# Moving a per-head multiplication from GpSimd to DVE, inverting in place, and normalizing a chunk earlier, in the projection of a gated DeltaNet layer

## The chip, the cores and the metric

One Trainium2 chip; the program runs on one core. The metric is device time in microseconds (us), the median of the runs shown. Layer 0, both expert layers and the final norm are in the same program as the part that is changed.

## The reference, cut to what matters

The model has two layers and a sequence of 2048 tokens with 1024 features. Layer 1 is a chunked gated DeltaNet with 8 heads of dimension 128. What the change touches is its first stage, up to the chunkwise scan:

```python
def gated_deltanet_mixer(h, w_in, conv_w, a_log, dt_bias, onorm_g, w_out):
    u = h @ w_in                                   # h = rmsnorm(x) * (1 + scale) + shift
    qkv = silu(causal_depthwise_conv(u[..., :3 * DN_WIDTH], conv_w))
    ...
    o = chunk_gated_delta_rule(l2norm(q), l2norm(k), v, beta, g)
    ...
def chunk_gated_delta_rule(q, k, v, beta, g):      # chunks of 64 tokens
    ...
    g = cumsum(g)                                  # within a chunk
    decay = where(causal, exp(g[:, None] - g[None, :]), 0)
    lower = where(strict, (k * beta) @ k.T * decay, 0)
    t_mat = triangular_solve(lower + eye, eye)     # the inversion
    u = t_mat @ (v * beta)
    w = t_mat @ (k * beta * exp(g))
    a_intra = where(causal, q @ k.T * decay, 0)
    qg = q * exp(g)
    kd = k * exp(g_last - g)
    ...                                            # scan over the chunks
```

## The kernel before, in words

`mixer1` runs `dn_project` and then `dn_chain`. `dn_project` makes, for all heads, what the scan needs, and stores it in HBM (the buffer `stg`); `dn_chain` loads it and scans. The sequence is worked off in two halves of 1024 tokens, and a half in two chunks of 512. For each chunk `norm_T` (L202 to L229) loads four tiles of x (128 tokens each, L1141), squares them on ScalarE (L212), makes the reciprocal root on DVE and GpSimd (`rstd`), scales the tiles on DVE (L219), transposes them on the tensor engine (L225), and splits the result into a high and a low part (nf L227, hh L228 on ScalarE, hl L229 on DVE), since every large product is done in three passes (high·high, high·low, low·high). Then `gates` makes beta and the decays of the half, ending in gh and gl (L1086) and in egd, an HBM copy of the cumulated exponentials.

After that `dn_head` (L1178 to L1297) runs for the 8 heads of the half:

- **Decays:** four products of the triangle `upper` with the head's column of g on GpSimd (gm, L1236, four buffers), each taken by the tensor engine (L1238) into a PSUM tile tk, ScalarE's exponential into dt (L1241) and a triangular mask on GpSimd (L1242).
- **Strips:** `strip(1)`, `strip(0)`, `strip(2)` project k, q and v: 48 matrix products of 128x512 each (L256 to L258), an eviction on ScalarE into ub (L1203), a causal filter of four taps on DVE (L1209, L1211, into dacc), and SiLU on ScalarE into kq (L1216; k and q side by side) or vT (L1214). The weights are split by ScalarE (wh) and DVE (wl, L234). After each strip `pump` emits two steps of an inversion, if one is under way, and a piece of the modulation of later layers (modw, mod; L168 and L169 on DVE).
- **Norms:** k and q are transposed by blocks (L1221), squared and summed; kd is made on DVE (L1261).
- **kg:** egb, the head's row of egd spread over all partitions, is loaded into the buffer that ub has used (L1267). kg = kq · egb is one GpSimd multiplication of 128x2048 (L1269), and is stored.
- **strip(3)** projects the output gate (zs, L1201).
- **The block of products:** for each of four pairs of 128-token blocks, kq is split (kqh on ScalarE, kql on DVE, L234), six products of 128x256 (L1281) fill a PSUM tile tp (two buffers), and DVE multiplies the tile by dt into na (L1282). na holds `lower` and `a_intra`. Its diagonal 32x32 pieces go to HBM (`ndia`), and the transposed v is evicted as vp (L1295).

After each four heads `dn_invert` (L1299 to L1318) inverts their diagonal pieces, 31 steps of a multiplication (L1312) and a sum (L1313) on DVE, which grow from 1 to 31 columns. Its generator is advanced by `pump`, two steps per strip, during the next four heads; the last one runs in `dn_chain`. The pieces are loaded into nblk, and the inverse grows in xblk; both come from the four buffers of the x tiles (tag "xin").

The order on each engine is not written out: a scheduler of the tile framework sets it from the program's order, the dependences and the buffers. The engines are in order, and so is SyncE (SP), which issues nearly all DMAs.

Of the kernel before, what the change touches and what calls it, by code (L numbers as in the profile page):

```python
# [6 lines left out]
F32 = mybir.dt.float32  # L7
F32R = mybir.dt.float32r
# [8 lines left out]
P = 128  # L17
# [53 lines left out]
class Trunk:  # L71
# [127 lines left out]
                nc.tensor.transpose(p[:, j * P:(j + 1) * P], src[:, k:k + 1].to_broadcast([P, P]), self.ident)  # L199
            nc.scalar.activation(out[:, h * 512:(h + 1) * 512], p, AF.Copy)  # L200

    def norm_T(self, l, which, xload, psum, wk, outs):  # L202


        nc = self.nc
        hh, hl = outs
        ss = self.small.tile([P, 4], F32, name="ss")
        xs = []
        for i in range(4):
            x = xload(i)  # L210
            sq = wk.tile([P, D], BF16, name="sq", tag="nf", bufs=2)
            nc.scalar.activation(sq, x, AF.Square, accum_out=ss[:, i:i + 1])  # L212
            xs.append(x)
        r = self.rstd(ss, 1.0 / D, 4, "rs")
        for i in range(4):
            if l == 0:
                nc.scalar.activation(xs[i], xs[i], AF.Copy, scale=r[:, i:i + 1])
            else:
                nc.vector.tensor_scalar(xs[i], xs[i], r[:, i:i + 1], None, op0=ALU.mult)  # L219
        g = self.gain[l, which]  # L220
        so = l * 48 + (0 if which == 0 else 3) * 8
        for k in range(KD):
            p = psum.tile([P, 512], F32, name="tp")
            for i in range(4):
                nc.tensor.transpose(p[:, i * P:(i + 1) * P], xs[i][:, k * P:(k + 1) * P], self.ident)  # L225
            f = wk.tile([P, 512], F32, name="nf", bufs=2)
            nc.scalar.activation(f, p, AF.Identity, scale=g[:, k:k + 1], bias=self.mod[:, so + k:so + k + 1])  # L227
            nc.scalar.activation(hh[:, k], f, AF.Copy)  # L228
            nc.vector.tensor_sub(hl[:, k], f, hh[:, k].bitcast(F32))  # L229
# [124 lines left out]
    def mixer0(self, yT, cv, gm):  # L354
        tc, nc, ins = self.tc, self.nc, self.ins
        cin = {}
        with ExitStack() as ctx:
# [4 lines left out]
            wk = ep("wk0", 2)  # L362
# [12 lines left out]
            def xload(c):  # L375
                return lambda i: x0[i] if c == 0 else self.xload0(wk, c * 4 + i)
# [10 lines left out]
            for half in range(2):  # L387
                hT = []
                for c2 in range(2):
                    hh = hp[c2].tile([P, KD, 512], F32R, name="hh")  # L390
                    hl = hp[c2].tile([P, KD, 512], F32R, name="hl")
                    self.norm_T(0, 0, xload(half * 2 + c2), pst, wk, (hh, hl))
                    hT.append((hh, hl))
                if half:
                    self.route_setup(wk)
# [718 lines left out]
    def dn_project(self):  # L1114
# [3 lines left out]
        with ExitStack() as ctx:  # L1118
# [24 lines left out]
                return f  # L1143

            self.rest = self.mod_rest(cv, [(1, i) for i in range(16, 48)], tag="modw", bufs=3)
            for half in range(2):
                hT = []
                ba = cv.tile([P, 8, 16], F32, name="ba", bufs=2)
                for c2 in range(2):
                    hh = hp.tile([P, KD, 512], F32R, name="hh")  # L1150
                    hl = hp.tile([P, KD, 512], F32R, name="hl")
                    self.norm_T(1, 0, xload(half * 2 + c2), pst, wk, (hh, hl))
                    hT.append((hh, hl))
                    p = psm.tile([P, 512], F32, name="pm")
                    self.proj(p[:16], (wbh, wbl), (hh, hl))
                    bs = wk.tile([16, 512], F32, name="bs", bufs=1)
                    nc.scalar.activation(bs, p[:16], AF.Copy)
                    p = pst.tile([P, 512], F32, name="tp")
                    for i in range(4):
                        nc.tensor.transpose(p[:, i * 16:(i + 1) * 16], bs[:, i * P:(i + 1) * P], self.ident[:16, :16])  # L1160
                    nc.vector.tensor_copy(ba[:, c2 * 4:c2 * 4 + 4], p[:, :64].rearrange("p (b c) -> p b c", b=4))
                beta, g, ex = self.gates(half, ba, cv, pst)
                for hd in range(8):
                    self.dn_head(half, hd, hT, beta, g, ex, halo, wp, wk, psm, pst, psk)
                    if hd % 4 == 3:
                        assert next(self.inv, None) is None
                        self.inv = self.dn_invert(half, hd // 4, wk) if (half, hd) != (1, 7) else iter(())
# [8 lines left out]
    def dn_head(self, half, hd, hT, beta, g, ex, halo, wp, wk, psm, pst, psk):  # L1176
# [55 lines left out]
        pe = psk.tile([P, 1024], F32, name="tk")  # L1232
        for c in range(2):
            for i in range(2):
                t = wk.tile([P, 4, P], F32R, name="gm", bufs=4)
                nc.gpsimd.tensor_mul(t, self.upper[:, None, :].to_broadcast([P, 4, P]),  # L1236
                                     g[i][:, hd, c * 4:c * 4 + 4, None].to_broadcast([P, 4, P]))
                nc.tensor.matmul(pe[:, c * 512:(c + 1) * 512], self.slower_r, t.rearrange("p b c -> p (b c)"),  # L1238
                                 start=i == 0, stop=i == 1)
# [25 lines left out]
        nc.gpsimd.tensor_tensor(self.fo[:, hd, half * 8:half * 8 + 8], ssq, self.expo[:, 0:1].to_broadcast([P, 8]), op=ALU.pow)  # L1265
        egb = wk.tile([P, 1024], F32, name="egb", tag="ub", bufs=1)
        nc.sync.dma_start(egb, self.egd[half][hd:hd + 1].to_broadcast([P, 1024]))  # L1267
        kg = self.last.tile([P, 8, 2, P], F32, name="kg", bufs=1)
        nc.gpsimd.tensor_mul(kg, kq, blk(egb)[:, :, None, :].to_broadcast([P, 8, 2, P]))  # L1269
        store(2, 2, kg)  # L1270
        strip(3)
        self.pump(2)
        na = self.last.tile([P, 8, 2, P], F32, name="na", bufs=1)
        for b in range(0, 8, 2):
# [4 lines left out]
            for i in range(2):  # L1279
                for n, (x, y) in enumerate(((kqh, kqh), (kqh, kql), (kql, kqh))):  # L1280
                    nc.tensor.matmul(p[:, i * 256:(i + 1) * 256], x[:, i, 0], y[:, i], start=n == 0, stop=n == 2)  # L1281
            nc.vector.tensor_mul(na[:, b:b + 2], p.rearrange("p (b i c) -> p b i c", b=2, i=2),  # L1282
                                 dt[:, b:b + 2, None, :].to_broadcast([P, 2, 2, P]))
        store(0, 2, na)
        nd, no = self.ndia[half][hd // 4], self.noff[half]
        for sub in range(4):
            dst = bass.AP(tensor=nd.tensor, offset=nd.offset + sub * 32768 + hd % 4 * 1024, ap=[[32, 32], [4096, 8], [1, 32]])
# [7 lines left out]
        nc.vector.tensor_mul(vp, pv, b8(nk))  # L1295
        store(5, 1, vp[:, :, None, :])

    def dn_invert(self, half, hg, wk, bufs=4):


        nc = self.nc
        n = wk.tile([P, 32, 32], F32, name="nblk", tag="xin", bufs=bufs)
        nc.sync.dma_start(n, self.ndia[half][hg])
        x = wk.tile([P, 32, 32], F32, name="xblk", tag="xin", bufs=bufs)
        nc.gpsimd.memset(x, 0.0)
        nc.gpsimd.memset(x.rearrange("p i j -> p (i j)")[:, 0:1024:33], 1.0)
        for j in range(1, 32):
            if j > 1:
                yield
            tmp = wk.tile([P, 32, 32], F32, name="xtmp", tag="sqk", bufs=1)  # L1310
            col = n[:, 0:j, j:j + 1].rearrange("p m o -> p o m").to_broadcast([P, j, j])
            nc.vector.tensor_mul(tmp[:, :j, :j], x[:, :j, :j], col)  # L1312
            nc.vector.tensor_reduce(x[:, 0:j, j:j + 1], tmp[:, :j, :j], axis=AX.X, op=ALU.add, negate=True)  # L1313
        nc.sync.dma_start(self.xinv[half][hg], x)
        xs = self.xsub[half]
        for sub in range(4):
            dst = bass.AP(tensor=xs.tensor, offset=xs.offset + hg * 4096 + sub * 1024, ap=[[8192, 32], [1, 1024]])
            nc.sync.dma_start(dst, x[sub * 32:(sub + 1) * 32].rearrange("p i j -> p (i j)"))  # L1318

    def dn_chain(self, yT):  # L1320
# [3 lines left out]
        with ExitStack() as ctx:  # L1324
# [196 lines left out]
            if True:  # L1521
                both = lambda bl: [load(bl, hg) for hg in range(2)]
                with tc.high_priority(offset=400):
# [2 lines left out]
                    load_n(1)  # L1526
                    both(1)
                    last = load_n(2)
                kg, zs, na, vp = self.stores[-4:]

                def behind(st, ld):
                    tc.add_manual_dep(st.ins, ld.ins.name,
# [10 lines left out]
                        run(*nxt)  # L1543
                for bl in range(16):
                    if bl == 0:
                        self.inv = self.dn_invert(1, 1, iv, 2)
                    if bl + 2 < 16:
                        last = both(bl + 2)[-1]
                    if bl == 0:
# [138 lines left out]
```

## Time and profile before

| | |
|---|---|
| median of 3 runs | 3399.24 us (3396.93 to 3402.08) |
| profiled execution: its time | 3396.98 us |
| profiled execution: span | 3395.2 us |
| mean granted TensorE clock | 0.929 of full speed |
| projection of layer 1 | about 1253 to 2280 us of the span |
| one head (k, q, v, gate strips and the block) | 52.0 to 58.3 us in the stretches read |

How the views are read: a timeline row has start and duration in us, engine, line of the kernel, operation, output<-input, shape, count, and in brackets the idle time of the engine before it with what ended it. PE is the tensor engine, PEld its weight loads, ACT is ScalarE, POOL GpSimd, SP SyncE. A row of waits has the waiting engine and instruction, the instruction waited for, and total us, number and longest. A row of groups has count, busy us and mean ns of one. A row by stretch has the busy time of each engine within it and the TensorE clock that was granted. Durations of matrix products overlap, so the distance from start to start tells their pace.

### The profile page before, as it was taken

Reading aid. Unit: us, or ns where it says so; the run is one execution under the profiler, and the core shown is the slowest. Engines: PE = TensorE matmul, PEld = TensorE weight load, DVE = VectorE, ACT = ScalarE, POOL = GpSimd, SP = SyncE. Lnnn points to the kernel's source line nnn. Section 1 sums busy time; section 2 is a strip of 40 time slices with the busy share of each in tenths; the row PEclk is TensorE's granted clock in tenths of the full one; section 3 lists DMA queues with packets and bytes.
Section 4 is the critical chain, followed back from the end, with each engine's and each line's share of the span. In section 5 each row is a group of like instructions: output and inputs, shape, how many; then the busy total and the mean of one; then the engine's idle time right before and its main releaser. Section 6 shows DMA issues by size and latency. Waiting matters only on the chain. (4 is left out here: it accounts for less than half of the span.)

```text
span 3395.2 us, 41934 instructions
## 1 busy us (share of the span) xinstructions
PE 2939.8 (87%) x14192; PEld 2344.0 (69%) x14192; DVE 2472.0 (73%) x3773; ACT 1492.9 (44%) x2558; POOL 1112.1 (33%) x897
## 2 busy tenths in 40 slices
PE   4979888869999978999878989988998996999991
PEld 3756666547777756877756777767896665777771
DVE  4998998758888856667867685777545656888883
ACT  6134223226565654334334333435663224656552
POOL 1143323333444413242313232244540122344331
PEclk9989989889999989999978999988998997999996
DMA  5216243729999852454432334348757535999875
GB/s 216 92 62 223 77 140 124 248 99 329 302 291 293 272 166 89 139 173 159 164 127 80 98 116 127 100 128 264 230 182 241 174 125 206 308 280 301 268 236 212
DMA packets 384987, 633.40 MB, mean 187 GB/s; under 512 B 111232, under 2 KB 245504, under 8 KB 384768
## 3 DMA queue, kind: packets, MB, share of 16 engines
q1 hardware_dynamic: 355904, 563.38, 48.8%
q0 software_dynamic: 28864, 67.30, 8.4%
q8 instruction: 114, 1.87, 0.2%
q14 instruction: 105, 0.86, 0.1%
HBM read 484.46 MB, written 175.44 MB: 194 GB/s over the span
## 5 line engine op out<-in xcount | busy, mean ns | idle before, releaser
L256 PE MATMUL pm<-hh,wh 128*128 128x512 f32 x1408 | 566.6, 403 | 4.5 <-ACT ub L1203 3.8
L257 PE MATMUL pm<-hl,wh 128*128 128x512 f32 x1408 | 555.6, 395 | 4.2 <-DVE hl L229 4.2
L258 PE MATMUL pm<-hh,wl 128*128 128x512 f32 x1408 | 555.9, 395 | 2.6 <-DVE wl L234 2.6
L234 DVE TENSOR_TENSOR wl<-wr,wh 128x1024 fp32r<-128x1024 f32 x384 | 452.1, 1218 | 41.5 <-ACT wh L233 37.3
L233 ACT ACTIVATE wh<-wr 128x1024 fp32r<-128x1024 f32 x384 | 399.4, 1057 | 126.2 <-PE pu L815 56.5
L834 POOL DMA_INDIRECT acc<-ys,ixs x102 | 264.0, 2588 | 436.4 <-DVE wl L234 132.6
L256 PEld LDWEIGHTS pm<-hh,wh 128*128 128x128 f32 x1408 | 270.3, 192 | 67.4 <-ACT ub L1203 6.3
L257 PEld LDWEIGHTS pm<-hl,wh 128*128 128x128 f32 x1408 | 269.6, 191 | 63.8 <-DVE hl L229 4.6
L258 PEld LDWEIGHTS pm<-hh,wl 128*128 128x128 f32 x1408 | 268.6, 191 | 61.9 <-DVE wl L234 4.7
L234 DVE TENSOR_TENSOR wl<-wraw,wh 128x1024 fp32r<-128x1024 f32 x88 | 133.8, 1520 | 186.6 <-ACT wh L233 186.6
L813 PE MATMUL pu<-wh,xt 128*128 128x512 f32 x656 | 268.6, 409 | 0.5 <-ACT xt L233 0.5
L814 PE MATMUL pu<-wl,xt 128*128 128x512 f32 x656 | 261.0, 398 | 0.0
L815 PE MATMUL pu<-wh,xt 128*128 128x512 f32 x656 | 260.0, 396 | 0.0
L282 DVE SCALAR_TENSOR_TENSOR acc<-cin,wfir,acc 128x512 f32<-128x512 f32 (+1 forms) x320 | 214.8, 727 | 0.1
L532 PE MATMUL po<-woh,yh 128*128 128x512 f32 x512 | 172.4, 413 | 31.5 <-issue 11.3
L1211 DVE SCALAR_TENSOR_TENSOR dacc<-ub,cols,dacc 128x1024 f32<-128x1024 f32 x144 | 188.9, 1312 | 3.0
L233 ACT ACTIVATE wh<-wraw 128x1024 fp32r<-128x1024 f32 x88 | 93.2, 1059 | 219.9 <-PE pm L257 219.8
L532 PE MATMUL po<-wol,yh 128*128 128x512 f32 x512 | 167.0, 406 | 0.0
L532 PE MATMUL po<-woh,yl 128*128 128x512 f32 x512 | 165.7, 403 | 0.2 <-DVE yl L234 0.2
L791 POOL DMA_INDIRECT xg<-hn,ixs x102 | 111.9, 1097 | 162.6 <-PE tp L801 76.5
L189 POOL TENSOR_TENSOR rs<-rs1t,expo 128x1 f32<-128x1 f32 x48 | 28.3, 589 | 383.7 <-DVE rs1t L187 354.6
L815 PEld LDWEIGHTS pu<-wh,xt 128*128 128x128 f32 x656 | 124.0, 189 | 30.8 <-issue 0.3
(377 smaller groups left out, 6520.1 us busy)
## 6 DMA issues: line engine op xcount, KB each, us to landing
wr<-in_w_up_dram SPq DMA_DIRECT2D x256, 512.0 KB
wr<-in_w_down_dram SPq DMA_DIRECT2D x128, 512.0 KB
modw<-in_modwT_dram SPq DMA_DIRECT2D x96, 512.0 KB
wraw<-in_w_in_dram SPq DMA_DIRECT2D x88, 512.0 KB
stin<-stg SPq DMA_DIRECT2D x32, 1280.0 KB
yr<-yT SPq DMA_DIRECT2D x32, 512.0 KB
acc<-xo SPq DMA_DIRECT2D x32, 512.0 KB
hn<-ho SPq DMA_DIRECT2D x32, 512.0 KB
```

The source lines that it names most:

```text
L233: a = nc.scalar.activation(h, x, AF.Copy) if eng == "act" else nc.vector.tensor_copy(h, x)
L234: return a, nc.vector.tensor_sub(l, x, h.bitcast(F32))
L256: nc.tensor.matmul(ps, wh[:, k], hh[:, k], start=k == 0, stop=False)
L257: nc.tensor.matmul(ps, wh[:, k], hl[:, k], start=False, stop=False)
L258: nc.tensor.matmul(ps, wl[:, k], hh[:, k], start=False, stop=k == KD - 1)
L282: self.tap = nc.vector.scalar_tensor_tensor(o, x, w, i, op0=ALU.mult, op1=ALU.add)
L532: nc.tensor.matmul(ps[:, ns], a[:, k], b[:, ns], start=k == 0 and i == 0, stop=k == KD - 1 and i == 2)
L813: nc.tensor.matmul(ps, xh[:, k], uh, start=k == 0, stop=False)
L814: nc.tensor.matmul(ps, xh[:, k], ul, start=False, stop=False)
L815: nc.tensor.matmul(ps, xl[:, k], uh, start=False, stop=k == KD - 1)
L834: st = nc.gpsimd.indirect_dma_start(out=self.acc, out_offset=bass.IndirectOffsetOnAxis(ap=ix[:, 0:1], axis=0), in_=ys, in_offset=None, bou ...
L1211: nc.vector.scalar_tensor_tensor(acc, ub[:, i:i + 1024], self.col("dn_conv", si * 4 + i), acc, op0=ALU.mult, op1=ALU.add)
```

## The change

It has five parts, all in or around `dn_project`.

1. `norm_T` is cut in two: `norm_x` (load, squares, root, scaling) and `norm_T` (transposes and split). For the first chunk of the second half `norm_x` is called before head 7 of the first half.
2. kg is made on DVE, in two multiplications of 128x1024, written behind the loop that makes na, and stored after na.
3. `dn_invert` works in place: the pieces are loaded straight into xblk, which gets a buffer of its own (one) instead of two of the four x tiles. The memset of the whole tile goes; the memset of the diagonal stays and now follows the load.
4. gm has two buffers instead of four.
5. `dn_chain` unpacks the last four stores in their new order (zs, na, kg, vp).

```diff
-    def norm_T(self, l, which, xload, psum, wk, outs):
+    def norm_x(self, l, xload, wk):
         nc = self.nc
-        hh, hl = outs
         ss = self.small.tile([P, 4], F32, name="ss")
...
                 nc.vector.tensor_scalar(xs[i], xs[i], r[:, i:i + 1], None, op0=ALU.mult)
+        return xs
+
+    def norm_T(self, l, which, xs, psum, wk, outs):
+        nc = self.nc
+        hh, hl = outs
...
+            first = None
             for half in range(2):
...
-                    self.norm_T(1, 0, xload(half * 2 + c2), pst, wk, (hh, hl))
+                    xs = first or self.norm_x(1, xload(half * 2 + c2), wk)
+                    first = None
+                    self.norm_T(1, 0, xs, pst, wk, (hh, hl))
...
                 for hd in range(8):
+                    if (half, hd) == (0, 7):
+                        first = self.norm_x(1, xload(2), wk)
                     self.dn_head(half, hd, hT, beta, g, ex, halo, wp, wk, psm, pst, psk)
...
-                t = wk.tile([P, 4, P], F32R, name="gm", bufs=4)
+                t = wk.tile([P, 4, P], F32R, name="gm", bufs=2)
...
-        kg = self.last.tile([P, 8, 2, P], F32, name="kg", bufs=1)
-        nc.gpsimd.tensor_mul(kg, kq, blk(egb)[:, :, None, :].to_broadcast([P, 8, 2, P]))
-        store(2, 2, kg)
         strip(3)
...
         store(0, 2, na)
+        kg = self.last.tile([P, 8, 2, P], F32, name="kg", bufs=1)
+        for b in range(0, 8, 4):
+            nc.vector.tensor_mul(kg[:, b:b + 4], kq[:, b:b + 4], blk(egb)[:, b:b + 4, None, :].to_broadcast([P, 4, 2, P]))
+        store(2, 2, kg)
...
-    def dn_invert(self, half, hg, wk, bufs=4):
+    def dn_invert(self, half, hg, wk):
         nc = self.nc
-        n = wk.tile([P, 32, 32], F32, name="nblk", tag="xin", bufs=bufs)
-        nc.sync.dma_start(n, self.ndia[half][hg])
-        x = wk.tile([P, 32, 32], F32, name="xblk", tag="xin", bufs=bufs)
-        nc.gpsimd.memset(x, 0.0)
+        x = wk.tile([P, 32, 32], F32, name="xblk", bufs=1)
+        nc.sync.dma_start(x, self.ndia[half][hg])
         nc.gpsimd.memset(x.rearrange("p i j -> p (i j)")[:, 0:1024:33], 1.0)
...
-            col = n[:, 0:j, j:j + 1].rearrange("p m o -> p o m").to_broadcast([P, j, j])
+            col = x[:, 0:j, j:j + 1].rearrange("p m o -> p o m").to_broadcast([P, j, j])
```

The scheduler turns this into other orders. The first place is DVE in the block of products of head 1 of the first half. Before (kd, na, wl the low weights of the next strip, kql the low part of k and q, vp):

```order
L1261 TENSOR_TENSOR kd<-tk,kdf 128x1024
L1282 TENSOR_TENSOR na<-tp,dt 128x512
L234 TENSOR_TENSOR wl<-wraw,wh 128x1024
L1282 TENSOR_TENSOR na<-tp,dt 128x512
L234 TENSOR_TENSOR kql<-kq,kqh 128x512 x2
L1295 TENSOR_TENSOR vp<-tk,nk 128x1024
L1282 TENSOR_TENSOR na<-tp,dt 128x512 x2
L234 TENSOR_TENSOR wl<-wraw,wh 128x1024
```

and now (lines from L203 on have moved: L1261 is L1270, L1282 is L1288, L234 is L238, L1295 is L1305, and L1293 is the new kg):

```order
L1270 TENSOR_TENSOR kd<-tk,kdf 128x1024
L1293 TENSOR_TENSOR kg<-kq,egb 128x1024 x2
L1288 TENSOR_TENSOR na<-tp,dt 128x512 x2
L238 TENSOR_TENSOR kql<-kq,kqh 128x512 x2
L1305 TENSOR_TENSOR vp<-tk,nk 128x1024
L1288 TENSOR_TENSOR na<-tp,dt 128x512 x2
L238 TENSOR_TENSOR wl<-wraw,wh 128x1024 x2
```

Both halves of kg stand ahead of the first na, although the program writes them behind the last, and wl stands behind the block.

The second place is the same engine in head 6, with the largest steps of the inversion (xtmp the multiplications, xblk the sums). Before:

```order
L1261 TENSOR_TENSOR kd<-tk,kdf 128x1024
L1313 TENSOR_REDUCE xblk<-xtmp 128x23
L169 TENSOR_TENSOR mod<-mod,cols 128x1
L1312 TENSOR_TENSOR xtmp<-xblk,nblk 128x24x24
L1313 TENSOR_REDUCE xblk<-xtmp 128x24
L1282 TENSOR_TENSOR na<-tp,dt 128x512 x2
L234 TENSOR_TENSOR kql<-kq,kqh 128x512 x2
L1295 TENSOR_TENSOR vp<-tk,nk 128x1024
L1282 TENSOR_TENSOR na<-tp,dt 128x512 x2
```

and now:

```order
L1270 TENSOR_TENSOR kd<-tk,kdf 128x1024
L1322 TENSOR_REDUCE xblk<-xtmp 128x23
L1293 TENSOR_TENSOR kg<-kq,egb 128x1024
L1321 TENSOR_TENSOR xtmp<-xblk 128x24x24
L1288 TENSOR_TENSOR na<-tp,dt 128x512
L1322 TENSOR_REDUCE xblk<-xtmp 128x24
L1288 TENSOR_TENSOR na<-tp,dt 128x512
L238 TENSOR_TENSOR kql<-kq,kqh 128x512 x2
L1293 TENSOR_TENSOR kg<-kq,egb 128x1024
L1288 TENSOR_TENSOR na<-tp,dt 128x512 x2
L1305 TENSOR_TENSOR vp<-tk,nk 128x1024
```

One half of kg and one multiplication of the inversion stand ahead of the first na there, the other half of kg ahead of the last two.

The third place is ScalarE at the start of the first half, where the decays of the half are made (gex and egT are the exponentials in `gates`, dt that of head 0, sq the squares of x tiles, ub the evictions of strips, ACT_TABLE_LOAD a change of function table). Before:

```order
L1203 ACTIVATE ub<-pm 128x512
L233 ACTIVATE wh<-wraw 128x1024
L1079 ACTIVATE gex<-tp 128x192
L1081 ACTIVATE egT<-tp 64x128
L1203 ACTIVATE ub<-pm 128x512
L1241 ACTIVATE dt<-tk 128x1024
L1216 ACT_TABLE_LOAD
L1216 ACTIVATE kq<-dacc 128x8x128
```

and now (L212 is L210, L233 is L237, L1079 is L1083, L1203 is L1212, L1216 is L1225, L1241 is L1250):

```order
L210 ACTIVATE sq,ss<-xin 128x1024 x2
L237 ACTIVATE wh<-wraw 128x1024
L1212 ACTIVATE ub<-pm 128x512
L1225 ACT_TABLE_LOAD
L1225 ACTIVATE kq<-dacc 128x8x128
L1212 ACTIVATE ub<-pm 128x512
L1083 ACT_TABLE_LOAD
L1083 ACTIVATE gex<-tp 128x192
L1085 ACTIVATE egT<-tp 64x128
L1250 ACTIVATE dt<-tk 128x1024
```

The squares of the second half's first chunk, written before head 7, stand here, and so do its four loads and four scalings on SyncE and DVE; the exponentials of the decays now come behind the first strip's SiLU and a further change of table.

More of the change, by code (lines that the diff above doesn't have):

```diff
@@ L391, in mixer0 @@
                     hl = hp[c2].tile([P, KD, 512], F32R, name="hl")
-                    self.norm_T(0, 0, xload(half * 2 + c2), pst, wk, (hh, hl))
+                    self.norm_T(0, 0, self.norm_x(0, xload(half * 2 + c2), wk), pst, wk, (hh, hl))
                     hT.append((hh, hl))
@@ L1528, in dn_chain @@
                     last = load_n(2)
-                kg, zs, na, vp = self.stores[-4:]
+                zs, na, kg, vp = self.stores[-4:]
                 def behind(st, ld):
@@ L1545, in dn_chain @@
                     if bl == 0:
-                        self.inv = self.dn_invert(1, 1, iv, 2)
+                        self.inv = self.dn_invert(1, 1, iv)
                     if bl + 2 < 16:
```

## The prediction, on record before the changed kernel was timed

> **What bounds the kernel now.** I read the page first, then the chain of waits over the projection of layer 1 (1280 to 2300 us), then a timeline of one head, then tables by stretch.
>
> ```profile
> span 3395.2 us, 41934 instructions
> PE 2939.8 (87%) x14192; PEld 2344.0 (69%) x14192; DVE 2472.0 (73%) x3773; ACT 1492.9 (44%) x2558; POOL 1112.1 (33%) x897
> ```
>
> TensorE is busy for 87% of the span, so a gain has to come out of its idle time or its clock. In the waits of the projection these rows touch what the change edits (columns: total us, times, longest us):
>
> ```profile
> PE tp L1281 <- DVE na L1282: 61.4, 15, 5.3
> PE tp L225 <- DVE xin L219: 20.0, 2, 14.2
> POOL kg L1269 <- DMA egb<-egd: 14.6, 14, 2.0
> ```
>
> TensorE waits 61.4 us in 15 waits for na, the eviction of the k·kᵀ and k·qᵀ products, and 14.2 us once for normalized x. Why na is late shows in the timelines of head 6 of the first half, TensorE first, then DVE, then GpSimd:
>
> ```profile
> 1676.50 0.39 PE L258 MATMUL pm<-hh,wl 128*128 128x512 f32 x1
> 1676.73 0.28 PE L1281 MATMUL tp<-kqh 128*128 128x256 f32 x1
> 1676.85 0.28 PE L1281 MATMUL tp<-kql,kqh 128*128 128x256 f32 x1
> ...
> 1678.16 0.71 PE L1221 MATMUL tk<-ident,vT 128*128 128x128 f32 x5
> 1684.08 0.55 PE L1281 MATMUL tp<-kqh 128*128 128x256 f32 x1 [5.22 <-DVE na L1282]
> ...
> 1686.57 0.41 PE L1281 MATMUL tp<-kql,kqh 128*128 128x256 f32 x1
> 1686.78 0.41 PE L1281 MATMUL tp<-kqh,kql 128*128 128x256 f32 x1
> ```
> ```profile
> 1677.13 4.37 DVE L169 TENSOR_TENSOR mod<-mod,cols 128x1 f32<-128x1 f32 x1
> ...
> 1683.26 1.28 DVE L1282 TENSOR_TENSOR na<-tp,dt 128x512 f32<-128x512 f32 x2
> ```
> ```profile
> 1676.95 4.54 POOL L1269 TENSOR_TENSOR kg<-kq,egb 128x2048 f32<-128x2048 f32 x1
> ```
>
> While GpSimd multiplies kg for 4.54 us, a DVE multiplication of one column (L169) takes 4.37 us and ends when kg ends. The group of that line, stretched ones included, has a mean of 335 ns:
>
> ```profile
> L169 DVE TENSOR_TENSOR mod<-mod,cols 128x1 f32<-128x1 f32 x28 | 9.4, 335 | 0.5
> ```
>
> Head 0 shows who is held (GpSimd, then DVE, then TensorE):
>
> ```profile
> 1341.67 4.58 POOL L1269 TENSOR_TENSOR kg<-kq,egb 128x2048 f32<-128x2048 f32 x1 [0.83 <-DMA egb<-egd]
> ```
> ```profile
> 1342.71 0.69 DVE L1282 TENSOR_TENSOR na<-tp,dt 128x512 f32<-128x512 f32 x1 [1.95 <-PE tp L1281]
> 1343.32 4.02 DVE L234 TENSOR_TENSOR wl<-wraw,wh 128x1024 fp32r<-128x1024 f32 x1
> 1347.26 0.68 DVE L1282 TENSOR_TENSOR na<-tp,dt 128x512 f32<-128x512 f32 x1
> 1347.86 1.07 DVE L234 TENSOR_TENSOR kql<-kq,kqh 128x512 fp32r<-128x512 f32 x1
> ```
> ```profile
> 1348.08 0.55 PE L1281 MATMUL tp<-kqh 128*128 128x256 f32 x1 [2.62 <-DVE na L1282]
> ```
>
> na reads PSUM and runs during kg at 0.69; wl has two SBUF inputs and is held until kg ends. DVE works in order, so the second na stands behind the held wl. With two PSUM buffers TensorE then stops for 2.62 us. It pays again afterwards: in head 6 the products stood 0.12 us apart before the gap and 0.21 behind it. The tables by stretch show the clock (a row has the stretch and its length, the busy time and count of PE, PEld, DVE, ACT and POOL, the granted clock, the DMA share and GB/s):
>
> ```profile
> 1347.90:1351.20 3.30, 3.12 (x11) 2.75 (x12) 3.30 (x4) 0.00 (x0) 3.30 (x3) 0.50 1.06 397
> 2241.10:2244.40 3.30, 3.30 (x15) 2.71 (x16) 2.45 (x3) 1.27 (x2) 0.69 (x1) 1.00 0.00 0
> ```
> ```profile
> 2240.99 0.50 PE L256 MATMUL pm<-hh,wh 128*128 128x512 f32 x1 [1.39 <-ACT ub L1203]
> ```
>
> Behind the gap of 2.62 us the granted clock is 0.50 for 3.3 us, which loses 1.65 us of work; behind one of 1.39 us it stays 1.00. So the cost of a block of products is its whole stretch, from the first product to the next strip. For the first 15 heads in one table:
>
> ```profile
> sum 168.20, PE 105.62 PEld 93.52 DVE 154.11 ACT 40.14 POOL 123.57; mean PE 7.04 PEld 6.23 DVE 10.27 ACT 2.68 POOL 8.24
> ```
>
> 168.2 / 15 = 11.2 us each. At full clock TensorE needs about 4.7 (my estimate): 24 products by 0.12, eight transposes by about 0.11 (five took 0.71 with the tail of the last), and four decay products (L1238) as wide as a strip's product, which is 0.23 from start to start (1676.50 to 1676.73).
>
> **The change part by part.** Prices first, from the groups of the projection, and for a DVE product of 1024 elements with two SBUF inputs from the page:
>
> ```profile
> L1269 POOL TENSOR_TENSOR kg<-kq,egb 128x2048 f32<-128x2048 f32 x16 | 73.9, 4617 | 14.8 <-DMA egb<-egd 14.6
> L234 DVE TENSOR_TENSOR kql<-kq,kqh 128x512 fp32r<-128x512 f32 x62 | 47.8, 811 | 23.2 <-ACT kqh L233 23.2
> L1312 DVE TENSOR_TENSOR xtmp<-xblk,nblk 128x961 f32<-128x961 f32 x3 | 5.9, 1959 | 0.0
> L219 DVE TENSOR_SCALAR xin<-xin,rs 128x1024 f32<-128x1024 f32 x8 | 5.5, 750 | 2.2 <-POOL rs L189 2.2
> ```
> ```profile
> L234 DVE TENSOR_TENSOR wl<-wr,wh 128x1024 fp32r<-128x1024 f32 x384 | 452.1, 1218 | 41.5 <-ACT wh L233 37.3
> ```
>
> *kg on DVE.* It removes 16 × 4.62 = 73.9 us from GpSimd and adds 32 multiplications of 1024 elements to DVE. The nearest row is wl, 1218 ns; the far end is the inversion's product, 1959 ns for 961 elements, or 2.09 us for 1024. I take 1.22, since kg reads whole rows as wl does, so 2.44 per head. The order puts both halves ahead of the first na in most heads, not behind the evictions. From kg's start the first na can therefore end after 2.44 + 0.69 = 3.1 us. kg starts near the first product (1676.95 against 1676.73). TensorE spends 12 × 0.12 = 1.4 us on two pairs and about 0.6 on five transposes, so it waits about 1.1 us. The second na ends at 3.8; two kql at 0.81 each bring the last operand to 5.4, some decay products of the next head fill in, and the last products and the rest end near 6.6 us. The gain per block is 11.2 − 6.6 = 4.6, and over 15 blocks 69.0 us.
>
> Two deductions. In heads 6, 10 and 14 the last and largest inversion steps share DVE; in the period of head 6 (second row) DVE has little left, beside a head without an inversion (first row):
>
> ```profile
> 1396.50:1452.90 56.40, 53.55 (x245) 44.39 (x244) 37.50 (x45) 21.47 (x32) 19.25 (x15) 0.94 0.46 153
> ...
> 1630.70:1689.00 58.30, 53.08 (x246) 44.62 (x246) 50.16 (x60) 21.48 (x32) 19.80 (x12) 0.94 0.45 151
> ```
>
> It is busy 50.16 of 58.3 us there, against 37.5 of 56.4. The hold that goes is 4.37 less the few tenths that L169 takes by itself, about 4.2; kg adds 2.44. Where DVE sets the pace the gain is the difference, 1.8, less the new mix of steps; I take 1.5 instead of 4.6, which is −9.3. Second, a gap of 1.1 us mostly keeps the clock, but where the DMA of egb lands late it grows towards 2.4. For a third of the blocks I charge a half-clock stretch: 5 × 1.7 = −8.5.
>
> In the Trainium skill, the page TensorE: Matmul & The Clock Gate, section HAM oscillation — how this bites in real kernels, puts the loss of the clock at idle gaps over about 3.4 us. The 2.62 us gap above contradicts it. By that rule the second deduction would be nil and the time 8.5 us lower.
>
> *The wait that is added.* DVE now waits in order for egb; GpSimd waited 14.6 us in 14 heads for it, 1.0 each. Behind it stand na, kql and vp, and TensorE waits for na. This is inside the 6.6, because kg starts in my count where it started before. The lower bound of this cost is nil, the upper is a rival below. The next head's ub (GpSimd's halo copy) shares egb's buffer and now waits for DVE's kg, which ends earlier than GpSimd's did.
>
> *Early normalization.* The half boundary shows
>
> ```profile
> 1765.44 2.58 PE L225 MATMUL tp<-ident,xin 128*128 128x128 f32 x8 [14.24 <-DVE xin L219]
> ```
> ```profile
> 1762.06 1.06 ACT L212 ACTIVATE sq<-xin 128x1024 bf16<-128x1024 f32 x1 [15.68 <-DMA xin<-acc]
> ```
>
> Two of the four x tiles were loaded only there; the inversion's two tiles come from the same four buffers. With x loaded, squared and scaled long before, the 14.24 us go. What is late next is ScalarE's nf and hh of the same chunk, already counted in the rest of that stretch. The order, however, moves this work much further than head 7: the loads, the four squares on ScalarE and the four scalings on DVE stand at the start of the first half, inside the chain that makes the decays. There TensorE already waits:
>
> ```profile
> 1306.86 0.50 PE L1238 MATMUL tk<-gm,slower_r 128*128 128x512 f32 x1 [1.25 <-POOL gm L1236]
> ```
>
> Four squares at 1.06 us and four scalings at 0.75 come to 7.2 us at most if all stand in the way; nothing if strips cover them. I take 5.0, near the upper end, since the first strips' FIR stages are also put into that chain.
>
> *In place inversion and two gm buffers.* One buffer and one full memset per inversion (three, on GpSimd, for which nothing waits) go; the diagonal memset waits for the load, with strips of 48 × 0.23 = 11 us as cover; uncovered it would be one DMA wait per inversion, three in all. The decay products now come one at a time; inside a block TensorE has free time for it, at the start it is in the 5.0. Both: nothing.
>
> *Sum:* 69.0 − 9.3 − 8.5 + 14.2 − 5.0 = 60.4 us. From the profiled execution's 3396.98 that leaves 3336.6; that execution lies 2.3 under the median of 3399.24 and inside the runs shown (3396.93 to 3402.08). I write 3337.
>
> **The rivals.** *A: kg on DVE is slow.* kql took 1.07 us in head 0, over its mean of 0.81. If kg's halves take 2.0 us (towards the inversion's price) each block is 1.6 longer and the gap, 2.7, costs the clock in all 12 lighter blocks: 12 × 1.6 + 7 × 1.7 = 31, so 3368. Against it: GpSimd's next work waits for kg, so little competes.
>
> *B: DVE sets the pace in every inversion head.* Eleven of the 15 blocks carry inversion steps. If the eight lighter ones also gain 1.8 instead of 4.6, 22 us are lost: 3359. For it: the order has inversion steps on both sides of na. Against: head 6 is the fullest of them, since the steps grow from 1 to 31 over four heads.
>
> *C: more.* No clock loss (8.5), no cost at the start (5.0), and the heavy heads like the others (up to 9.3) would give 3336.6 − 22.8 = 3314. The skill's rule of 3.4 us, cited above, is on this side.
>
> *D: slower.* egb's load is late: DVE is in order, so each microsecond of later landing is one in each of 16 heads. The gain is used up at 60.4 / 16 = 3.8 us later than now; at 4.5 us the time is 3336.6 + 72 = 3409. For it: egb can load only after the FIR stage has read ub, behind other issues of SyncE. Against: the waits of GpSimd are 2.0 at the longest, and nothing earlier in that chain moves.
>
> *E: no change.* kg on DVE holds na as long as the lock did, half of the boundary's 14.2 goes into ScalarE's work on the same chunk, and the start takes its 5.0: 3395. Against it: 2.44 is well under 4.58.
>
> **How the numbers follow.** Forecast 0.59 (own range 3320 to 3352), A 0.12, B 0.12, C 0.10, D 0.04, E 0.03. The range from 3310 to 3370 leaves out D, E and the tails of A and C. A difference of 0.2%, about 7 us, is what a measurement of this kernel can tell from none: faster 0.93, same 0.03, slower 0.04.
>
> **What would show it.** Right: L169 and wl near their usual length beside the block, kg as 32 DVE rows near 1.22 us, the wait of TensorE for na near 15 to 20 us instead of 61, the block stretches near 6.6 us, no 14 us gap at the half boundary. Wrong: kg rows near 2 us (A), DVE without idle time in heads 4 to 14 and na still late (B), DVE waiting for egb by 4 us and more (D), or a TensorE gap of over 8 us at the first half's decays.

## The result and the profile after

| | before | changed |
|---|---|---|
| median | 3398.09 us (3395.29 to 3402.08, 4 runs) | 3317.52 us (3314.58 to 3321.46, 4 runs) |
| profiled execution: time, span | 3396.98, 3395.2 us | 3314.58, 3312.9 us |
| mean granted TensorE clock | 0.929 | 0.943 |

The ratio is 0.9764 (95% interval 0.9751 to 0.9777): 80.6 us less, where 60.4 were forecast. The time lies inside the forecast range of 3310 to 3370, but below the 3320 to 3352 that the forecast gave to its own sum.

In the waits of the projection, the rows that answer to those of before (TensorE's own, and the new wait of GpSimd for kg):

```profile
POOL ub L1205 <- DVE kg L1293: 41.3, 10, 5.5
...
PE tk L1230 <- ACT kq L1225: 17.0, 4, 7.1
...
PE tp L1287 <- DVE na L1288: 10.8, 15, 1.3
PE tk L1247 <- POOL gm L1245: 9.6, 14, 1.5
...
PE tp L229 <- DVE xin L217: 6.2, 1, 6.2
```

The wait for na fell from 61.4 to 10.8 us, and the longest from 5.3 to 1.3. The wait at the half boundary is gone; the 6.2 left is that of the second chunk, about 5.8 before. Two waits grew; before they were

```profile
PE tk L1221 <- ACT kq L1216: 7.5, 2, 4.1
...
PE tk L1238 <- POOL gm L1236: 3.0, 4, 1.2
```

The 17.0 us for kq in four heads stand out now. The groups on DVE show what became of the held instructions and what kg costs there:

```profile
L238 DVE TENSOR_TENSOR wl<-wraw,wh 128x1024 fp32r<-128x1024 f32 x62 | 76.4, 1233 | 140.6 <-ACT wh L237 140.6
...
L1293 DVE TENSOR_TENSOR kg<-kq,egb 128x1024 f32<-128x1024 f32 x32 | 39.9, 1272 | 4.9 <-DMA egb<-egd 4.9
...
L169 DVE TENSOR_TENSOR mod<-mod,cols 128x1 f32<-128x1 f32 x28 | 4.5, 162 | 0.5
```

L169 went from a mean of 335 ns to 162. kg takes 1272 ns in the mean, most of its multiplications 1.22 us, and DVE waits 4.9 us in all for egb. The block of products in head 0, on DVE and then the gaps of TensorE:

```profile
1343.05 2.36 DVE L1293 TENSOR_TENSOR kg<-kq,egb 128x1024 f32<-128x1024 f32 x2 [1.13 <-DMA egb<-egd]
1345.33 1.28 DVE L1288 TENSOR_TENSOR na<-tp,dt 128x512 f32<-128x512 f32 x2
1346.52 2.18 DVE L238 TENSOR_TENSOR kql<-kq,kqh 128x512 fp32r<-128x512 f32 x2
```
```profile
1346.15 0.36 PE L1287 MATMUL tp<-kqh 128*128 128x256 f32 x1 [0.57 <-DVE na L1288]
...
1348.76 0.39 PE L1287 MATMUL tp<-kql,kqh 128*128 128x256 f32 x1 [0.59 <-DVE kql L238]
```

Two gaps of under 0.6 us stand where one of 2.62 stood, and behind them the clock is kept. The table of the 15 blocks, from the first product to the next strip (the rows of heads 0 and 6; the clock is the figure before the DMA share), first before:

```profile
1341.70:1351.70 10.00, 7.38 (x40) 6.25 (x39) 8.99 (x7) 2.58 (x4) 9.94 (x6) 0.83 0.62 211
...
1676.70:1689.00 12.30, 7.08 (x37) 6.56 (x36) 10.88 (x11) 2.58 (x4) 5.84 (x3) 0.73 0.61 205
```

and now, with the sum:

```profile
1342.90:1349.60 6.70, 5.54 (x39) 4.69 (x38) 6.55 (x7) 2.54 (x4) 3.96 (x4) 1.00 0.92 312
...
1655.50:1663.30 7.80, 6.74 (x44) 5.63 (x43) 7.80 (x11) 2.75 (x5) 3.42 (x4) 1.00 0.43 137
...
sum 107.40, PE 84.99 PEld 71.03 DVE 106.01 ACT 38.74 POOL 55.68; mean PE 5.67 PEld 4.74 DVE 7.07 ACT 2.58 POOL 3.71
```

107.4 / 15 = 7.2 us a block instead of 11.2, which is 60.8 us, and the clock is 1.00 in all 15. At the half boundary the transposes of x now follow the block at once:

```profile
1723.28 1.25 PE L229 MATMUL tp<-ident,xin 128*128 128x128 f32 x8 [0.88 <-DVE na L1288]
```

Read from one first product of a block to the next, the stretch of head 7 with the boundary took 110.5 us before and 90.2 now. Its block became 4.9 shorter (10.3 to 5.4), so the boundary itself gave 15.4. From the first block to the last it was 923.0 us and is 845.5. The first block starts 1.2 us later than before (1342.9 against 1341.7), and from the last block's start to the end of the program it is 6.0 us less (1130.5 to 1124.5). That makes 77.5 − 1.2 + 6.0 = 82.3, the difference of the spans.

### The profile page after: what moved, and what is told of

Same layout as the page of the kernel before. It is cut to its first block, busy times and chain, and to the rows that moved or that the text cites. A ratio compares the mean times of both kernels' runs of the same rounds, so it can differ in the third digit from the quotient of the medians.

```text
span 3312.9 us, 41950 instructions
## 1 busy us (share of the span) xinstructions
PE 2905.9 (88%) x14192; PEld 2311.3 (70%) x14192; DVE 2440.1 (74%) x3805; ACT 1495.6 (45%) x2560; POOL 1023.9 (31%) x877
## 5 line engine op out<-in xcount | busy, mean ns | idle before, releaser
L238 DVE TENSOR_TENSOR wl<-wr,wh 128x1024 fp32r<-128x1024 f32 x384 | 452.0, 1217 | 41.6 <-ACT wh L237 38.4
L237 ACT ACTIVATE wh<-wr 128x1024 fp32r<-128x1024 f32 x384 | 399.4, 1057 | 126.4 <-PE pu L819 57.2
L238 DVE TENSOR_TENSOR wl<-wraw,wh 128x1024 fp32r<-128x1024 f32 x88 | 110.9, 1260 | 152.1 <-ACT wh L237 152.0
L536 PE MATMUL po<-woh,yh 128*128 128x512 f32 x512 | 172.7, 414 | 30.6 <-issue 10.7
L237 ACT ACTIVATE wh<-wraw 128x1024 fp32r<-128x1024 f32 x88 | 93.2, 1059 | 224.5 <-PE pm L261 224.3
## 6 DMA issues: line engine op xcount, KB each, us to landing
stin<-stg SPq DMA_DIRECT2D x32, 1280.0 KB, 10.5
```

Source lines behind the costliest of these rows:

```text
L237: a = nc.scalar.activation(h, x, AF.Copy) if eng == "act" else nc.vector.tensor_copy(h, x)
L238: return a, nc.vector.tensor_sub(l, x, h.bitcast(F32))
L536: nc.tensor.matmul(ps[:, ns], a[:, k], b[:, ns], start=k == 0 and i == 0, stop=k == KD - 1 and i == 2)
```

## The experiments

Two theories stood against each other at first. H: the GpSimd multiplication holds DVE's instructions with two SBUF inputs, and this makes na late. B: the boundary and the freed buffers carry most of it. In each comparison below the kernel before ran on the same chip. Its median was 3401.13 beside the two runs with added GpSimd work and the one with the inversion's steps behind the filter, 3400.73 beside the last three runs, and 3400.02 beside the others. Beside the changed kernel it was 3398.09, so medians from different chips differ by some 3 us without any change; where that matters, the ratios decide.

**kg back on GpSimd, all else as changed.**

```diff
         nc.sync.dma_start(egb, ...)
+        nc.gpsimd.tensor_mul(kg, kq, blk(egb)[:, :, None, :].to_broadcast([P, 8, 2, P]))
+        store(2, 2, kg)
...
-        for b in range(0, 8, 4):
-            nc.vector.tensor_mul(kg[:, b:b + 4], kq[:, b:b + 4], ...)
-        store(2, 2, kg)
...
```

> The changed kernel with one part undone: kg is again one GpSimd multiplication of 128x2048 ahead of the gate strip. The in place inversion, the two gm buffers and the early normalization stay. Theory H (GpSimd's kg holds DVE's operations with two SBUF inputs, so na is late and TensorE waits and loses its clock): the waits of TensorE for na come back to about 60 us and the time rises by some 60 from 3317.5, to 3378 (3365 to 3390). Theory B (most of the gain is the half boundary and the freed x buffers): it stays under 3340.

3383.31 us (ratio 0.9956, 0.9941 to 0.9971). The wait for na is back at its old size, and in head 6 the multiplication of one column on DVE is held again:

```profile
PE tp L1290 <- DVE na L1291: 61.2, 16, 5.4
```
```profile
1677.97 4.35 DVE L169 TENSOR_TENSOR mod<-mod,cols 128x1 f32<-128x1 f32 x1
```

Against the changed kernel that is 65.8 us, the worth of moving kg; against the kernel before it is 16.7, the worth of the rest. H holds, B falls.

**Only kg moved, all else as before.**

```diff
-        nc.gpsimd.tensor_mul(kg, kq, blk(egb)[:, :, None, :].to_broadcast([P, 8, 2, P]))
-        store(2, 2, kg)
...
         store(0, 2, na)
...
+        for b in range(0, 8, 4):
+            nc.vector.tensor_mul(kg[:, b:b + 4], kq[:, b:b + 4], ...)
+        store(2, 2, kg)
...
```

> The kernel before with one part of the change: kg on DVE in two multiplications; inversion, gm buffers and normalization as before. Theory H: 3398 less some 61, about 3337 (3325 to 3345), with the 14 us gap at the half boundary still there. Theory B: little, 3375 or more. If the two parts add, this run and the one with kg back on GpSimd leave about 80 us together.

3336.50 us (ratio 0.9811, 0.9796 to 0.9826), 63.5 less than before. The gap at the boundary is still there, longer even:

```profile
PE tp L225 <- DVE xin L219: 29.4, 3, 17.6
...
PE tp L1278 <- DVE na L1279: 10.3, 15, 1.0
```

63.5 and 16.7 add to 80.2 of the 80.6. The rest of the change is thus worth 16.7 us, and one step of it can be told without a run. If only the early call of `norm_x` is taken back, the order that the scheduler gives all five engines stays the same, instruction for instruction: with these buffers it moves these loads, squares and scalings to the start of the first half from either place. So the 16.7 us come from the inversion in place and the two gm buffers. What frees the x tiles is the inversion's own buffer; its 4 KB per partition are just the two gm tiles given up. No run times these two apart.

**One more GpSimd multiplication, and memsets in its place.** Each adds its work to the changed kernel at the old place of kg, with modw in two buffers to make room. The first reads SBUF, the second only writes; nobody uses the tile.

```diff
+        with self.tc.issue_after(fo.ins):
+            nc.gpsimd.tensor_mul(dm, kq[:, 0:4], blk(egb)[:, 0:4, None, :].to_broadcast([P, 4, 2, P]))
```
```diff
+        with self.tc.issue_after(fo.ins):
+            for _ in range(3):
+                nc.gpsimd.memset(dm, 0.0)
```

> The changed kernel with one more GpSimd multiplication per head, 128x1024 of kq and egb into a tile that nobody reads, at the place where kg was (modw has two buffers instead of three, to make room). It is half of the old kg, some 2.3 us. Theory H (a GpSimd operation that reads SBUF holds DVE's operations with two SBUF inputs): kg's first half on DVE starts some 2.3 us later, TensorE's wait for na grows from about 0.7 to about 3 and costs the clock: 25 to 60 us more than 3317.5. Theory G (GpSimd's load by itself, its place in front of gm, is what counts): the same as with the three memsets of the run beside it.

> The same place and about the same length on GpSimd (three memsets of 128x1024 at about 0.95 us), but nothing is read (modw has two buffers instead of three). Theory H: DVE is not held, na stays where it is, within 6 us of 3317.5; gm comes a little later, which may cost up to 10. Theory G: as much as the multiplication of the run beside it. Theory W (any GpSimd operation on SBUF holds DVE): 25 to 60 us more.

With the multiplication 3363.44 us (0.9886, 0.9871 to 0.9901), with the memsets 3322.92 (0.9771, 0.9756 to 0.9786). The views by tile give count, least, median and greatest duration (ns) of the added work and of kg on DVE, and the waits give TensorE's; first with the multiplication:

```profile
L1279 POOL TENSOR_TENSOR dm<-kq,egb x16: 2378/2604/3411, 1345.4 to 2230.9; 128x1024 f32<-128x1024 f32 x16
```
```profile
L1296 DVE TENSOR_TENSOR kg<-kq,egb x32: 1210/2377/3450, 1345.3 to 2234.4; 128x1024 f32<-128x1024 f32 x32
```
```profile
PE tp L1290 <- DVE na L1291: 42.0, 15, 3.7
```

and then with the memsets:

```profile
L1280 POOL MEMSET dm<- x48: 947/954/961, 1344.0 to 2193.6; 128x1024 f32 x48
```
```profile
L1297 DVE TENSOR_TENSOR kg<-kq,egb x32: 1209/1221/2061, 1345.1 to 2193.7; 128x1024 f32<-128x1024 f32 x32
```
```profile
PE tp L1291 <- DVE na L1292: 10.0, 15, 1.0
```

2.6 us of multiplying per head stretch kg on DVE to a median of 2.38 us, bring the wait for na to 42.0 us and cost 46 us by the medians, about 41 by the ratios; 2.9 us of memsets stretch nothing, leave that wait at 10.0 and cost 5 by the medians, 2 by the ratios, whose intervals overlap. The memsets did lie beside kg: 22 of its 32 rows overlap one by 0.69 us or more, and the longest of these takes 1.24 us. In the other run the 16 rows that lie beside the multiplication and began after it take 2.70 to 3.45 us. What holds DVE is GpSimd reading SBUF beside an instruction with two SBUF inputs, not GpSimd being busy. The Trainium skill says the same on its page SBUF — State Buffer, under Who interferes with whom: two SBUF inputs contend with a GpSimd instruction that reads SBUF, not with one that only writes it.

**kg truly behind the evictions.** The scheduler had put it ahead of them.

```diff
-            nc.vector.tensor_mul(na[:, b:b + 2], ...)
+            nal = nc.vector.tensor_mul(na[:, b:b + 2], ...)
...
+        with self.tc.issue_after(nal.ins):
             for b in range(0, 8, 4):
```

> The changed kernel with kg's two multiplications bound behind the last na of the block on DVE. TensorE's waits for na are 10.8 us in 15 times in the changed kernel. Theory N (kg ahead of na costs what these waits show, up to 1.3 a head): 3306 to 3311. Theory O (the waits only move: wl or kql take the place, and the next head's ub, which shares egb's buffer, is free later): no difference within 4 us of 3317.5, or some us slower.

3327.01 us (0.9787, 0.9774 to 0.98): some 8 us more than the changed kernel by the ratios, 9 by the medians, and the two intervals just touch. The wait for na hardly moved (10.2 us), and the last block starts at 2188.3, as with kg ahead (2188.4), so within the projection nothing is won. The loss that the trace shows lies behind it, in the start of the chain. There are DVE's kg of the last head, the chain's first load of the stored tiles, and TensorE:

```profile
2206.13 3.42 DVE L1294 TENSOR_TENSOR kg<-kq,egb 128x1024 f32<-128x1024 f32 x2
```
```profile
2209.62 2.28 SPq L1389 DMA_DIRECT2D stin<-stg  x4
```
```profile
2209.86 1.94 PE L1447 MATMUL mm<-x2t,nd 128*128 128x64 f32 x8 [4.29 <-issue]
```

That product reads x2t, and DVE's copy into x2t stands behind kg and starts at 2209.48. With kg ahead, kg ran at 2188.5, the load was issued at 2206.6, and the gap was 0.94. The first product with a loaded tile comes 36.0 us after the last block's start instead of 29.7: 6.3 of the 10.7 by which the stretch to the end is longer (1135.2 against 1124.5). In these traces kg's place ahead of the evictions is thus the better one, if only for the last head. The other 4.4 us lie in later parts, where the kernel before is also 4.6 us longer than the changed one.

**The transposes of k behind the strip.** This and the next four runs go after the 17.0 us that TensorE now waits for kq.

```diff
-        pk = tok(lambda b: kq[:, b, 0])
+        with self.tc.issue_after(self.lastmm.ins):      # the v strip's last product
+            pk = tok(lambda b: kq[:, b, 0])
```

> The changed kernel with the transposes of k bound behind the v strip's last product on TensorE, where the scheduler had put some of them ahead of that strip in four heads; there TensorE waits 17.0 us in all for ScalarE's kq. Theory Q (the order of TensorE costs these waits, and the strip would cover them): 17 us and a few more of clock less, 3295 to 3300. Theory D (DVE is late with the filter in these heads because of the largest inversion steps, and TensorE would wait a strip later for the same reason): 3312 to 3318.

3323.71 us (0.9778, 0.9764 to 0.9793): no gain. It is 6 us above the changed kernel and outside both ranges, but the intervals of the ratios overlap. The same waits stand a strip later, at the products that need the PSUM tile of an eviction which is itself queued behind kq on ScalarE:

```profile
PE pm L260 <- ACT ub L1212: 17.4, 4, 7.1
```

The cause is not TensorE's order. In head 6 of the changed kernel DVE shows it; after the filter (dacc) come ScalarE's table load and kq, and TensorE's gap ends at 1690.76:

```profile
1677.07 1.74 DVE L1321 TENSOR_TENSOR xtmp<-xblk 128x841 f32<-128x841 f32 x1
1678.85 1.03 DVE L1322 TENSOR_REDUCE xblk<-xtmp 128x29 f32<-128x841 f32 x1
1679.91 1.86 DVE L1321 TENSOR_TENSOR xtmp<-xblk 128x900 f32<-128x900 f32 x1
1681.69 0.73 DVE L1218 TENSOR_SCALAR dacc<-ub,cols 128x1024 f32<-128x1024 f32 x1
```
```profile
1688.36 1.28 ACT L1225 ACT_TABLE_LOAD   x1 [3.76 <-DVE dacc L1220]
1689.65 1.06 ACT L1225 ACTIVATE kq<-dacc 128x1024 f32<-128x1024 f32 x1
```
```profile
1690.76 0.69 PE L1230 MATMUL tk<-ident,kq 128*128 128x128 f32 x2 [7.08 <-ACT kq L1225]
```

**The inversion's steps behind the filter.**

```diff
-        for _ in range(n):
-            next(self.inv, None)
+        with self.tc.issue_after(self.fir.ins):         # the strip's last filter tap
+            for _ in range(n):
+                next(self.inv, None)
```

> The changed kernel with the inversion's steps bound behind the filter of the strip ahead of them on DVE. In the changed kernel TensorE waits 17.0 us in four heads (7.1, 3.2, 3.3, 3.4) for kq, and binding the transposes of k behind the strip only moved these waits to the next strip. Theory D (DVE is late with the filter because steps of the inversion stand ahead of it): the four waits go, with their clock some 20 us less, 3295 to 3302. Theory F (DVE has no time to spare in these heads): the waits move to na or to kql, and the time stays within 6 us of 3317.5. kg stands ahead of the k norms in the fullest heads of this order, so DVE may also wait there for egb's load, which would show as a wait of kg for that DMA of 2 us and more.

3320.94 us (0.9761, 0.9748 to 0.9774): no difference. The waits moved to the squares and to na:

```profile
PE tp L1288 <- DVE na L1289: 8.3, 5, 6.7
PE tk L1231 <- ACT sqk L1236: 8.3, 4, 3.6
...
PE tk L1231 <- ACT kq L1226: 7.9, 1, 7.9
...
DVE kg L1294 <- DMA egb<-egd: 5.7, 8, 1.1
```

egb is not what DVE waits for. It has too much to do there: F. The stretches from block to block say it too: those of heads 6, 10 and 14 fall from 61.6, 58.3 and 58.5 us to 52.9, 52.8 and 52.5, but the one with the half boundary grows from 90.2 to 100.0 and that of head 11 from 55.9 to 66.2. The inversions now end inside these two stretches (at 1722.9 and 1980.3 us, with the blocks begun at 1710.6 and 1968.5), so DVE's work has moved and not gone.

**No kg at all.** The multiplication is left out and kq is stored in kg's place.

```diff
-        for b in range(0, 8, 4):
-            nc.vector.tensor_mul(kg[:, b:b + 4], kq[:, b:b + 4], ...)
-        store(2, 2, kg)
+        store(2, 2, kq)
```

> The changed kernel without kg's multiplication: kq is stored in its place, so the queries and keys are not weighted by their decays; the same bytes are stored. It shows what the 39.9 us of kg on DVE still cost. Theory F (DVE is full at the end of each inversion, and elsewhere kg lies beside TensorE's work): the four waits for kq shrink by about 2.4 us each, some with their clock, 3300 to 3312. Theory N (kg ahead of na costs in every head): 16 heads by 0.7 and more, 3295 to 3306, with the period of a head without inversion under the 51.8 us of the changed kernel.

3303.44 us (0.9714, 0.9701 to 0.9728), 14 us under the changed kernel for 39.9 us of DVE work. Of the waits for kq one of four is left:

```profile
PE tk L1230 <- ACT kq L1225: 3.9, 1, 3.9
```

From block to block a head without an inversion takes 51.8 us with kg and 51.8 without, so there it is hidden. The gain lies near the ends of the inversions: the stretches of heads 6, 11 and 14 shrink from 61.6, 55.9 and 58.5 to 59.2, 51.8 and 54.8. That of head 10 does not (58.3 to 58.5), and the one with the boundary grows by 2.1. The profiled execution is the slowest of its five runs, so these stretches show less than the 14 us.

**The steps spread by size.** Two ways: alone, and bound behind the filter as well.

```diff
-        for _ in range(n):
+        for _ in range((12, 3, 2, 2, 2, 1, 1, 1, 1, 1, 1, 1, 1, 1, 1, 1)[self.turn % 16]):
             next(self.inv, None)
+        self.turn += 1
```

> The changed kernel with the inversion's 31 steps spread by their size over the 16 strips (12, 3, 2, 2, 2 steps and then one at a time) instead of two per strip. Theory F (DVE is full only where the largest steps come two per strip): the four waits for kq in heads 6, 10, 11 and 14 go, 17 us and some clock, 3295 to 3305. Rival: the scheduler puts the steps in front of the filter elsewhere, its order has transposes of k ahead of the strip in ten heads instead of five, and the waits come back in others, 3310 to 3330.

> The steps spread by size as in the run beside it, and bound behind the filter of the strip ahead of them on DVE. Theory F: both causes of a late filter are gone, the waits for kq go, 3292 to 3302. Rival: kg now stands ahead of the norms of k in many heads, so DVE waits there for egb's load, and squares and transposes are late instead: 3310 to 3330.

Alone 3306.32 us (0.9724, 0.9706 to 0.9742); with the binding 3310.26 (0.9742, 0.9727 to 0.9757). Both are faster than the changed kernel's 0.9764 in the middle, the first with an interval that lies apart from its 0.9751 to 0.9777. Of the waits for kq 0.3 us is left in the first one; what remains of na:

```profile
PE tp L1289 <- DVE na L1290: 10.9, 12, 2.1
```

The stretch of head 6 falls from 61.6 to 52.7 us, those of heads 10 and 14 from 58.3 and 58.5 to 53.9 and 53.1. Head 4, which now gets 12 steps at once, gives back 3.4 (52.6 to 56.0), and the one with the boundary 3.3 (90.2 to 93.5). This version beats both kernels, by 11 us the changed one. It missed F's range by 1 us. With the binding the time falls into the range of its rival; head 11 takes 58.1 us there, against 51.6 without the binding, and TensorE waits for kq once, 3.3 us.

## Why the prediction was right, and where its sizes were off

- **The mechanism** (GpSimd's kg holds DVE, DVE is in order, na is late, TensorE waits and then runs at half clock) is shown, by putting kg back and by the two loads on GpSimd.
- **The block, 69.0 − 9.3:** 59.7 us forecast without the clock, 60.8 measured in the 15 blocks. That these agree is in part luck. The 12 lighter blocks gave 49.8 where 55.2 were forecast: those of the four heads without an inversion (0 to 3) began from 10.0 to 10.5 us, less than the mean of 11.2, and end at 6.7 to 6.8, near the forecast 6.6; five with steps of an inversion (heads 4, 5, 9, 12 and 13) end at 7.4 to 7.6. The three fullest (heads 6, 10 and 14) gave 4.5, 3.2 and 3.3, together 11.0, where 4.5 were forecast. kg was priced at 1.22 us and takes 1.22 in most rows. The runs that move kg alone give 63.5 to 65.8 in all.
- **The clock, −8.5:** this is the mis-sized step. No block loses the clock: after the change no gap in a block is over 1.5 us, and 1.00 was granted in all 15. The forecast feared gaps growing to 2.4 from a late egb, but DVE waits for it 4.9 us in all.
- **Heads 6, 10 and 14, −9.3:** too much in the blocks, right in kind from block to block, where the gain is 2.7, 3.6 and 0.9 instead of the 1.5 each that was forecast for the block. In heads 6 and 14 part of what the block gained was lost again behind it, where TensorE waits for kq. DVE being full there is what the last runs show, and a better spread of the steps gets 11 us back.
- **The boundary, +14.2:** 15.4 in the stretches and 16.7 as the whole rest of the change. But the reason given was half right: the freed tiles count, and with them the early call does nothing.
- **In place inversion and two gm buffers, 0:** the first is what frees the tiles, so its worth is in the boundary. For gm TensorE now waits 9.6 us in 14 times instead of 3.0 in 4; none is over 1.5. What that costs is not measured by itself.
- **The start, −5.0:** not paid. The first block begins 1.2 us later, and the first gap of the projection already opens 1.1 us later (1235.2 against 1234.1). The moved squares and scalings cost next to nothing.
- **The end, +6.0, not forecast:** 1.7 of it by the end of the chain; the rest is in parts that the change does not touch, and the same stretch took 1123.9 to 1135.2 us in the other runs. It stays open how much of it belongs to the change.

The profiled executions differ by 82.3 us, 21.9 more than the sum: 9.6 in the blocks (8.5 for the clock, 6.5 for the three fullest, less 5.4 for the others), 1.2 at the boundary, 3.8 at the start (−1.2 instead of −5.0), 6.0 at the end and 1.3 between the blocks. Rival A (slow kg) and D (late egb) are refuted by the rows of kg and its wait, B by the blocks of the eight lighter inversion heads (3.6 to 5.4 us gained each, not 1.8) and by stretches such as those of heads 8 and 9 (57.2 and 57.8 before, 51.7 and 52.2 after), E by the time. C, which had a chance of 0.10, came nearest in time: 3314 with no clock loss, no cost at the start and lighter heavy heads. The first came true, the second nearly (1.2 us), the third in the blocks alone.

## What to carry to other kernels

An engine that is far from full can still set the pace through what it holds: look for short instructions that take as long as a neighbour's long one and end with it. When such a wait is removed, count the idle gap that is left against the length that costs the clock in your own traces, and charge no clock below it. Ask the built order before believing where a line is written: here kg, written behind the evictions, was placed ahead of them, the early call of `norm_x` changed nothing in the order, and forcing kg behind the evictions gained nothing.

## What the runs showed of the hardware

- **How long a gap costs the clock.** Over six of the profiles I took the gaps of TensorE in and around the projection with no other gap near, and the clock granted in the 3.4 us behind each. Of 27 gaps from 0.82 to 1.69 us, 25 were followed by 1.00 (the others by 0.65 and 0.79). Of 54 from 2.38 to 7.6 us, 53 were followed by 0.72 or less, 33 of them by 0.50. The step lies between 1.7 and 2.4 us here; the rule of 3.4 us from the Trainium skill (TensorE: Matmul & The Clock Gate, HAM oscillation — how this bites in real kernels) does not fit these rows.
- **What GpSimd may do beside DVE.** 2.6 us of multiplying per head cost 41 to 46 us, 2.9 us of memset 2 to 5, the latter within the spread of the runs.
- **Who is held.** In five heads of the run with the added multiplication kg's first half began 0.04 to 0.05 us ahead of it. That half took 1.23 us, and the multiplication took 3.40 to 3.41 instead of the 2.38 to 2.72 of the other heads; the second half, begun beside the multiplication, took 3.39 to 3.40. In these rows the one that began first ran at its usual pace, and the other waited for it.
